# Two convolution layers of a diffusion trunk: the order of the input projection's tiles, and the output projection block by block

## The chip, the core and the metric

The kernel runs on one core of one Trainium2 chip. The metric is device time in microseconds (us) of one execution; lower is better. Three runs of the kernel before took 3041.77, 3048.72 and 3049.2 us, median 3048.72. One execution more was profiled; everything called a row below is from it.

## The reference

Four layers are applied to 1152 tokens (128 context tokens, then a latent grid of 16 x 64), 1024 channels each. Layer i takes mixer i mod 3, so layers 0 and 3 are convolution layers, layer 1 is an attention layer, layer 2 a state space layer. The change touches layers 0 and 3 alone. All data is float32.

```python
h = rms_norm(x, norm_w) * (1 + scale) + shift        # shift, scale, gate: silu(cond) @ ada_w + ada_b
v, g, z = split(h @ w_in + b_in, 3)                  # 1024 x 3072
u = v * sigmoid(g)
u = depthwise_conv(u, w_dw, b_dw)                    # 31 taps along the tokens; context and latent apart
u = silu(layer_norm(u, ln_w, ln_b))                  # over the 1024 channels of a token
y = (u * silu(z)) @ w_out + b_out                    # 1024 x 1024
x = x + gate * y
```

After layer 3 a last RMSNorm gives the outputs.

## The kernel before, in words

Channels lie on partitions, 128 at a time (a tile m, 0 to 7), tokens along the free axis in three blocks of 384. A float32 product is made of three matmuls on two-part operands (hi x hi, lo x hi, hi x lo). A *unit* (`unit`, L511 to L520) is one 128-channel output tile for one block: 8 row tiles x 3 matmuls = 24 matmuls of 128x384 (L517, L518, L519) into one buffer of the PSUM pool `mm`, which has three. The weights come 128 columns (512 KB) at a time: a load on SP's DMA queue (L464, three `raw` buffers), then ScalarE writes the high part `wh` (L478) and GpSimd the low part `wl` (L479), two buffers each, one tile ahead of use (`ahead`).

**Input projection of a convolution layer.** For every m there is a g tile, a v tile and a z tile, three units each. ScalarE takes the sigmoid of g (L662), VectorE multiplies it with v out of PSUM into `u` (L670; three `u` buffers in turn), ScalarE writes silu(z) (L684), and each z tile goes to DRAM (`zd`). After v of tile m, its depthwise convolution is put on a list of small steps: 21 taps on VectorE, accumulating in PSUM (`ca`: L819, then L821), 10 taps on ScalarE and GpSimd (`pa`: L809, L813, L814), and the sum of both (`c`, L830). After each unit `tick` writes the next steps of the list into the program. Buffer `u` of tile m is written again by tile m + 3. In layer 0, 32 columns of `ada_w` (the modulation of this and of the next layer) stand between the tiles (`ada_tile`: 16 + 2 small matmuls each; L281 and L284 on VectorE).

`TAIL` sets where z stands: g0 v0 g1 v1 g2 v2 z0 g3 v3 z1 ... g7 v7 z5 z6, and z7 beside the LayerNorm. The convolution of the last tile is cut into its three blocks, so that the LayerNorm of block 0 can start before blocks 1 and 2 are convolved; those go on between the LayerNorm's steps.

**LayerNorm and gate** (`conv_norm`, L750 to L784), a block at a time: sum over channels by matmuls with ones (L692), mean, difference (L766, even tiles on VectorE, odd ones on GpSimd), square (L768), its sum (L769), the reciprocal root by a dozen tiny VectorE operations (L368 to L376), then for each channel tile two VectorE operations (L777, L780, the second with z read back from DRAM, L775), two on ScalarE (L779, L781) and one on GpSimd (L782). The result is the pair `gh`, `gl`.

**Output projection** (`out_proj`, L620 to L638): for the pair of blocks (0, 1), then for block 2, over m: take the weight tile, load the old x (`xm`, L631; in layer 0 all 1152 tokens of the tile, as they are reordered for layer 1), one unit per block, then scale and bias (L602, ScalarE), add (L611, VectorE) and the sum of squares (L340 ScalarE, L341 GpSimd). So the 8 weight tiles come twice a layer. When a group's blocks are done, the next layer's norm of them starts (in layer 3: three transposes a unit, L1586 and L1588, and the final norm).

**What sets the order.** Every engine runs its own queue in a fixed order. That order is made when the program is built: a planner plays the program through on a timeline of its own; the written order is the priority, and an instruction whose inputs or buffers are not there yet can be passed by a later one.

Of the kernel before, what the change touches and what calls it, by code (L numbers as in the profile page):

```python
# [9 lines left out]
F32 = mybir.dt.float32  # L10
# [9 lines left out]
P = 128  # L20
# [16 lines left out]
POOL_LAST = 10, 10  # L37
# [32 lines left out]
TAIL = {0: TAIL0, 3: TAIL3}  # L70


REST = 4
TURN_ACT = (1,), (1,), (0, 1)
VAR_MM = 2


# Columns of the projection of a pair of heads (0: q, 1: k, 2: v, 3: the gate), in three parts.
# [11 lines left out]
def conv_order(l):  # L90
    """The order of the tiles of a convolution layer: (v, g, z) and the columns of ada_w put in between."""
    ada = [("ada", 0, i) for i in range(2 * KT, 3 * KT)] if l == 0 else []
    ada += [("ada", l + 1, i) for i in range(3 * KT)] if l + 1 < DEPTH else []
    out = []
    n = len(ada)
    for m in range(KT):
        out += [("g", m), ("v", m)] + [("z", z) for z in TAIL[l][0][m]]
    tiles = len(out) - 1
    res = out[:1]
    for i, t in enumerate(out[1:]):  # L100
        res.append(t)
        res += ada[i * n // tiles:(i + 1) * n // tiles]
    return res
# [6 lines left out]
# The latent grid has 16 rows of 64 columns. Besides the row order, its tokens are kept in the order of 8 groups of  # L110
# 8 columns, row by row within a group, where every block of 8 x 16 keys or queries is a run of 128 tokens.
# [5 lines left out]
def cols_of_rows(a, b):  # L117
    """The tokens of block b of the column order, from a, the latent tokens in row order."""
# [3 lines left out]
def rows_of_cols(a, b):  # L122
    """The tokens of block b of the row order, from a, the latent tokens in column order."""
# [3 lines left out]
def like(order, a, b):  # L127
    """The latent part of block b, in the shape that order gives."""
# [5 lines left out]
def interleave(a, na, b, nb):  # L134
    """Runs two generators side by side, na and nb steps of them spread evenly, to the end of both."""
# [11 lines left out]
def part(gen, n):  # L147
    """The next n steps of a generator."""
# [12 lines left out]
def also(a, b, n=1):  # L161
    """Generator a, with n steps of b after each of its own."""
# [6 lines left out]
class Kern:  # L169
    def __init__(self, ctx, tc, A, O, depth):  # L170
# [13 lines left out]
        self.h = [None] * NB  # L184
        self.ada_end = lambda: None
# [78 lines left out]
    def ada_tile(self, l, i):  # L264
        """Column i of the 24 of layer l."""
# [77 lines left out]
    def rstd(self, acc, n, eps, times=1.0):  # L343
        """times / sqrt(sum over partitions of acc / n + eps) on every partition."""
# [7 lines left out]
    def rstd_row(self, row, n, eps):  # L352
        """1 / sqrt(row / n + eps) on every partition, of a row that is the same on all of them."""
# [9 lines left out]
    def rsqrt(self, x, n, eps):  # L363
        """1 / sqrt(x / n + eps) of a [128, 3] operand, by Newton's iteration."""
# [14 lines left out]
    def spread(self, y, times=1.0):  # L379
        """y [128, 3], a value per token, as a row of 384 tokens on every partition."""  # L380
# [34 lines left out]
    # All of them stream through the same buffers in the order of their use, loads and splits ahead of it.  # L415
    def weight_specs(self):
# [5 lines left out]
        for l in range(self.depth):  # L422
            kind, j = l % 3, l // 3
            if kind == 0:
# [7 lines left out]
                out += [(w, 2 * D + z * P, P) for z in TAIL[l][1]]  # L432
# [19 lines left out]
            if kind != 2:  # L452
                out += [(w, m * P, P) for g in range(2) for m in range(KT)]
# [29 lines left out]
    def ahead(self, i):  # L483
        """Loads what follows, and splits the next that is to be split."""
# [26 lines left out]
    def unit(self, out, w, h, width=P, first=True, last=True):  # L511
        """out [width, 384] = w^T h over 8 row tiles."""
# [13 lines left out]
    def tick(self):  # L526
        for _ in range(STEPS_A_UNIT):
# [34 lines left out]
    def hb(self, h, b):  # L562
        """Block b of the normed input h of a layer, what is left of its computation first."""
# [56 lines left out]
    def out_proj(self, l, g, bias=None, order=None):  # L620
# [27 lines left out]
    def conv_layer(self, l, j, order, hook=None):  # L648
        nc, tc, h = self.nc, self.tc, self.h
        with tc.tile_pool(name="cp", bufs=1, space=PSUM, reuse_waits="tile") as cp, ExitStack() as stack:  # L650
            cw = stack.enter_context(tc.tile_pool(name="cw", bufs=2, reuse_waits="tile"))
            close = stack.close
            up = [cw.tile([P, ULEN], F32, name=f"u{i}", bufs=1) for i in range(3)]
# [1060 lines left out]
```

## Time and profile before

| | |
|---|---|
| runs | 3041.77, 3048.72, 3049.2 us (median 3048.72) |
| profiled execution | span 3039.6 us from the first to the last instruction; no other time of that execution is given, so 9.1 us below the median is what lies around the span, and the difference between executions |
| busy share of the span | TensorE 92%, VectorE 72%, GpSimd 48%, ScalarE 44% |
| layer 0 | g and v units from 60.4 us, output projection from 451.8, layer 1's first unit at 596.7 |
| layer 3 | first unit at 2531.9 us, output projection from 2879.1, its last matmul ends at 3025.2, end at 3039.6 |

How to read it: the windows view gives, for a stretch of the span, each engine's busy time with its count of instructions, then the TensorE clock that was granted (1.00 is 2.4 GHz, 0.50 is 1.2 GHz), the busy share of the 16 DMA engines and what they moved. Busy TensorE is not TensorE at its peak, since matmuls overlap; counts of matmuls tell more.

### The profile page before, as it was taken

What the parts mean: (1) busy time and instruction counts of PE and PEld (TensorE: products, weight loads), DVE (VectorE), ACT (ScalarE), POOL (GpSimd) and SP (SyncE); (2) the same over time, 40 slices, a digit from 0 to 9 for tenths busy, and PEclk for the clock granted to TensorE, in tenths of its full rate; (3) what the DMA queues carried; (4) which work ended last, traced back from release to release, by engine and by line L of the source; (5) the groups of instructions that cost most, each with busy time, mean ns of one, the idle gap of its engine ahead of it and who ended that gap; (6) DMA issues with size and microseconds to landing.
All of it is one profiled execution on the core that took longest, in us unless ns stands there. A gap on an engine that the chain in (4) does not pass through costs nothing. (4 is left out here: it accounts for less than half of the span.)

```text
span 3039.6 us, 47664 instructions
## 1 busy us (share of the span) xinstructions
PE 2806.9 (92%) x18263; PEld 2579.5 (85%) x18263; DVE 2174.9 (72%) x3297; ACT 1337.5 (44%) x2293; POOL 1447.8 (48%) x815
## 2 busy tenths in 40 slices
PE   7989988899999999998999999788788999999877
PEld 5979977889999998797999988677677889999677
DVE  5878897754455445557887678987997575999975
ACT  5545555443333334444433334333443444555553
POOL 1767766511111010353134335755675446888764
PEclk7989999999999999998999999999889999999999
DMA  6555424733322333363345579756787863111234
GB/s 215 196 190 153 125 89 128 236 89 92 87 76 75 88 86 86 118 191 112 92 145 165 165 231 289 221 185 211 239 258 223 251 187 96 53 58 56 75 102 137
DMA packets 548643, 445.99 MB, mean 147 GB/s; under 512 B 26944, under 2 KB 506176, under 8 KB 548416
## 3 DMA queue, kind: packets, MB, share of 16 engines
q1 hardware_dynamic: 530704, 422.22, 45.7%
q10 hardware_dynamic: 17712, 20.73, 2.1%
q8 instruction: 144, 2.36, 0.3%
q14 instruction: 83, 0.68, 0.1%
HBM read 337.44 MB, written 101.09 MB: 144 GB/s over the span
## 5 line engine op out<-in xcount | busy, mean ns | idle before, releaser
L479 POOL TENSOR_TENSOR wl<-raw,wh 128x1024 fp32r<-128x1024 f32 x169 | 409.4, 2424 | 959.0 <-ACT wh L478 934.0
L821 DVE SCALAR_TENSOR_TENSOR ca<-u,vec,ca 128x1167 f32<-128x1167 f32 (+4 forms) x420 | 481.4, 1146 | 11.4
L814 POOL TENSOR_TENSOR pa<-pa,pt 128x1167 f32<-128x1167 f32 (+4 forms) x189 | 399.9, 2118 | 87.0 <-ACT pt L813 44.6
L478 ACT CAST wh<-raw 128x1024 fp32r<-128x1024 f32 (+1 forms) x239 | 249.3, 1043 | 313.1 <-issue 61.1
L517 PE MATMUL in_ps<-hh,wh 128*128 128x384 f32 x768 | 268.2, 351 | 4.5 <-ACT hh L408 2.1
L519 PE MATMUL in_ps<-hh,wl 128*128 128x384 f32 x768 | 262.0, 341 | 0.0
L518 PE MATMUL in_ps<-hl,wh 128*128 128x384 f32 x768 | 261.4, 340 | 0.7 <-DVE hl L409 0.7
L813 ACT ACTIVATE pt<-u,vec 128x1167 f32<-128x1167 f32 (+4 forms) x189 | 193.9, 1038 | 108.9 <-POOL pa L814 105.2
L517 PE MATMUL op<-gh,wh 128*128 128x384 f32 x576 | 203.8, 356 | 13.0 <-ACT gh L781 11.0
L1365 DVE SCALAR_TENSOR_TENSOR sca<-ub,vec,sca 128x1155 f32<-128x1155 f32 x144 | 204.9, 1423 | 3.5
L517 PE MATMUL x_ps<-hh,wh 128*128 128x384 f32 x576 | 205.1, 356 | 1.3 <-ACT ub L1316 0.7
L518 PE MATMUL op<-gl,wh 128*128 128x384 f32 x576 | 202.6, 352 | 2.0 <-POOL gl L782 2.0
L519 PE MATMUL op<-gh,wl 128*128 128x384 f32 x576 | 200.9, 350 | 2.2 <-POOL wl L479 2.2
L519 PE MATMUL x_ps<-hh,wl 128*128 128x384 f32 x576 | 197.3, 343 | 0.1
L518 PE MATMUL x_ps<-hl,wh 128*128 128x384 f32 x576 | 196.0, 340 | 0.0
L517 PEld LDWEIGHTS in_ps<-hh,wh 128*128 128x128 f32 x768 | 145.1, 189 | 14.5 <-issue 4.2
L341 POOL TENSOR_TENSOR ssq<-ssq,sq 128x384 f32<-128x384 f32 x84 | 92.6, 1104 | 122.4 <-ACT sq L340 119.2
L519 PE MATMUL op<-sgh,wl 128*128 128x384 f32 x384 | 135.3, 352 | 16.9 <-DVE wl L479 10.9
L518 PEld LDWEIGHTS in_ps<-hl,wh 128*128 128x128 f32 x768 | 145.3, 189 | 2.9 <-DVE hl L409 0.9
L519 PEld LDWEIGHTS in_ps<-hh,wl 128*128 128x128 f32 x768 | 145.2, 189 | 3.1 <-issue 2.4
L611 DVE TENSOR_TENSOR xr<-nt,xm 128x384 f32<-128x384 f32 (+2 forms) x72 | 84.2, 1185 | 85.0 <-ACT nt L605 50.8
L519 PE MATMUL sz_ps<-hh,wl 128*128 128x384 f32 x384 | 137.0, 357 | 7.0 <-DVE wl L479 6.9
(291 smaller groups left out, 8055.0 us busy)
## 6 DMA issues: line engine op xcount, KB each, us to landing
raw<-in_ada_w SPq DMA_DIRECT2D x96, 512.0 KB, 5.1
raw<-in_ssd_w_in SPq DMA_DIRECT2D x62, 512.0 KB, 4.6
raw<-in_conv_w_in SPq DMA_DIRECT2D x48, 512.0 KB, 3.7
raw<-in_ssd_w_out SPq DMA_DIRECT2D x48, 512.0 KB, 4.8
xm<-xs SPq DMA_DIRECT2D x32, 576.0 KB, 4.2
rw<-ssd_rows SPq DMA_DIRECT2D x36, 512.0 KB, 6.6
raw<-in_conv_w_out SPq DMA_DIRECT2D x32, 512.0 KB, 4.1
raw<-in_na_w_in SPq DMA_DIRECT2D x32, 512.0 KB, 4.1
```

The costliest lines, as they stand in the source:

```text
L341: nc.gpsimd.tensor_tensor(out=acc, in0=acc, in1=sq, op=ALU.add)
L478: nc.scalar.copy(out=wh[:, :, :width], in_=s)
L479: self.w_eng.tensor_tensor(out=wl[:, :, :width], in0=s, in1=wh[:, :, :width].bitcast(F32), op=ALU.subtract)
L517: nc.tensor.matmul(out, lhsT=wh[:, k, :width], rhs=hh[:, k, :], start=f, stop=False)
L518: nc.tensor.matmul(out, lhsT=wh[:, k, :width], rhs=hl[:, k, :], start=False, stop=False)
L519: nc.tensor.matmul(out, lhsT=wl[:, k, :width], rhs=hh[:, k, :], start=False, stop=l)
L611: nc.vector.tensor_tensor(out=o, in0=i, in1=x, op=ALU.add)
L813: nc.scalar.activation(out=pt, in_=u_t, func=AF.Copy, scale=wt(t))
L814: nc.gpsimd.tensor_tensor(out=p, in0=p, in1=pt, op=ALU.add)
L821: nc.vector.scalar_tensor_tensor(out=c, in0=u_t, scalar=wt(t), in1=c, op0=ALU.mult, op1=ALU.add)
L1365: nc.vector.scalar_tensor_tensor(out=ca, in0=u[:, t:t + SCLEN], scalar=wt(t), in1=ca, op0=ALU.mult, op1=ALU.add)
```

## The change

In both convolution layers:

1. All g and v tiles come first (with layer 0's `ada_w` columns between them), and the eight z tiles after v7.
2. Six steps instead of four are written into the program after a unit (`CONV_STEPS`), back to four once the list is empty.
3. The last tile's convolution is no longer cut into blocks. The first part of the LayerNorm of all three blocks (sums, differences, squares) stands between z units, the second part of block 0 beside the last seven z units, that of blocks 1 and 2 beside the output projection. All three sums of squares lie in the PSUM space of `ca`. Block 0's pair `gh`, `gl` gets space of its own, and its last z tile is taken from SBUF.
4. The output projection goes block by block, (0), (1), (2): the 8 weight tiles are loaded and split three times instead of twice, and `xm` of a tile comes three times. `xm` uses the buffers of the g and z tiles.

```diff
-TAIL0 = ([(), (), (0,), (1,), (2,), (3,), (4,), (5, 6)], (7,), 0, 10)
-TAIL3 = ([(), (), (0,), (1,), (2,), (3,), (4,), (5, 6)], (7,), 1, 10)
+CONV_STEPS = 6
+LN_STEPS = 2
+Z_LAST = 7
 def conv_order(l):
...
     for m in range(KT):
-        out += [("g", m), ("v", m)] + [("z", z) for z in TAIL[l][0][m]]
+        out += [("g", m), ("v", m)]
...
-    return res
+    return res + [("z", z) for z in range(KT)]
 # weight_specs
-                out += [(w, m * P, P) for g in range(2) for m in range(KT)]
+                out += [(w, m * P, P) for g in range(3 if kind == 0 else 2) for m in range(KT)]
 # out_proj
-            for grp in ((0, 1), (2,)):
+            for grp in grps:
...
-                        xm[m] = pool.tile([P, x1 - x0], F32, name="xm", tag="xm", bufs=2)
+                        if xmp is None:
+                            xm[m] = pool.tile([P, x1 - x0], F32, name="xm", tag="xm", bufs=2)
+                        else:
+                            xm[m] = xmp.tile([P, T], F32, name="xm", tag="sg", bufs=2)[:, :x1 - x0]
 # conv_layer
+            self.steps_a_unit = CONV_STEPS
+            zs = []
...
-                    first, *rest = self.dwconv(cw, cp, u, cb, j, m, order, split=(m == KT - 1))
-                    self.steps += first
+                    self.steps += self.dwconv(cu, cp, u, cb, j, m, order)
...
                 elif t[0] == "z":
-                    for _ in z_tile(m):
-                        pass
+                    zs.append(z_tile(m))
...
-            rest = run(chain(*rest))
-            lns[0] = also(lns[0], rest, REST)
-            z, nz = chain(*[z_tile(m) for m in TAIL[l][1]]), NB * len(TAIL[l][1])
-            interleave(part(z, TAIL[l][2]), TAIL[l][2], part(lns[0], 9), 9)
-            for _ in rest:
-                pass
-            lns[0] = also(lns[0], part(lns[1], 9))
-            interleave(part(lns[0], TAIL[l][3]), TAIL[l][3], z, nz - TAIL[l][2])
-            self.flush()
-            close()
+            z, nz = chain(*zs), KT * NB
+            while self.steps:
+                next(z)
+                nz -= 1
+            self.steps_a_unit = STEPS_A_UNIT
...
             with tc.tile_pool(name="lz", bufs=3, reuse_waits="tile") as self.lz:
+                g0 = [self.lz.tile([P, KT, BW], F32R, name=f"g{i}0", bufs=1) for i in "hl"]
+                g = [None] * NB
+                self.var = cp.tile([P, 3 * 512], F32, name="var", tag="ca", bufs=1)
+                lns = [self.conv_norm(b, j, cb[b], s1, sums, zd, g, cp, g0 if b == 0 else None) for b in range(NB)]
+                firsts = chain(*(part(n, 1 + KT + LN_STEPS) for n in lns))
+                interleave(part(z, nz - Z_LAST), nz - Z_LAST, firsts, NB * (1 + KT + LN_STEPS))
+                interleave(z, Z_LAST, part(lns[0], KT + LAG - LN_STEPS - 1), KT + LAG - LN_STEPS - 1)
+                self.flush()
                 for _ in lns[0]:
                     pass
                 self.gens += lns[1:]
-                self.out_proj(l, g, bias=("conv_b_out", j * KT), order=order)
+                self.out_proj(l, g, bias=("conv_b_out", j * KT), order=order, grps=((0,), (1,), (2,)), xmp=cw)
 # conv_norm
+            if b == 0 and k == KT - 1:
+                z = self.zlast[:, :BW]
+            else:
...
```

## Rows read from the trace of the kernel before

**Rows 1.** The page: span, and busy time with its share of the span and instructions.

```profile
span 3039.6 us, 47664 instructions
...
PE 2806.9 (92%) x18263; PEld 2579.5 (85%) x18263; DVE 2174.9 (72%) x3297; ACT 1337.5 (44%) x2293; POOL 1447.8 (48%) x815
```

**Rows 2.** Windows: stretch, length, busy PE PEld DVE ACT POOL, clock, DMA share, GB/s.

```profile
60.40:451.80 391.40, 368.15 (x2394) 341.25 (x2392) 329.63 (x413) 202.83 (x282) 267.09 (x135) 0.97 0.46 143
451.80:596.70 144.90, 123.70 (x634) 115.63 (x634) 106.19 (x160) 76.58 (x144) 95.24 (x65) 0.93 0.57 177
2531.90:2879.10 347.20, 335.23 (x1823) 318.29 (x1822) 304.27 (x329) 192.74 (x234) 271.54 (x127) 0.99 0.19 58
2879.10:3039.60 160.50, 129.90 (x700) 121.15 (x700) 104.01 (x173) 71.15 (x124) 91.74 (x63) 0.89 0.41 129
```

**Rows 3.** Windows: shorter stretches of both layers.

```profile
158.70:197.50 38.80, 27.83 (x162) 24.62 (x162) 25.24 (x25) 18.08 (x20) 24.97 (x10) 0.78 0.66 211
220.80:263.20 42.40, 42.40 (x295) 40.55 (x293) 37.24 (x37) 23.12 (x26) 33.39 (x14) 1.00 0.56 162
2703.30:2742.00 38.70, 38.70 (x221) 38.17 (x221) 34.76 (x31) 22.34 (x23) 31.49 (x12) 1.00 0.19 62
2838.00:2879.10 41.10, 30.54 (x105) 19.11 (x104) 37.80 (x64) 24.70 (x48) 27.18 (x24) 0.92 0.06 20
552.80:594.00 41.20, 35.03 (x179) 33.00 (x179) 33.73 (x67) 20.96 (x39) 23.24 (x13) 0.92 0.76 240
2988.10:3025.20 37.10, 34.55 (x203) 33.98 (x202) 24.71 (x42) 15.94 (x22) 21.53 (x13) 0.95 0.55 179
3025.20:3039.60 14.40, 1.72 (x13) 1.18 (x11) 4.95 (x17) 2.34 (x3) 0.99 (x1) 0.64 0.27 110
```

**Rows 4.** Timeline of VectorE, one tile's convolution in layer 3: start, duration, instruction, idle before.

```profile
2779.45 1.55 DVE L830 TENSOR_TENSOR c<-ca,pa 128x128 f32<-128x128 f32 x4
2781.03 1.44 DVE L819 TENSOR_SCALAR ca<-u,vec 128x1167 f32<-128x1167 f32 x1
2782.51 14.70 DVE L821 SCALAR_TENSOR_TENSOR ca<-u,vec,ca 128x1167 f32<-128x1167 f32 x10
2798.95 0.74 DVE L670 SCALAR_TENSOR_TENSOR u<-v_ps,vec,sg 128x128 f32<-128x128 f32 x2 [1.75 <-PE v_ps L519]
```

**Rows 5.** Timeline of VectorE, the first tap of each layer.

```profile
88.54 1.44 DVE L819 TENSOR_SCALAR ca<-u,vec 128x1167 f32<-128x1167 f32 x1
...
2560.13 1.44 DVE L819 TENSOR_SCALAR ca<-u,vec 128x1167 f32<-128x1167 f32 x1
```

**Rows 6.** Timeline of VectorE in layer 3's LayerNorm, the last tile's taps beside it.

```profile
2855.14 0.67 DVE L371 TENSOR_SCALAR nr_y<-nr_y 128x3 int32<-128x3 int32 x1
2855.72 0.61 DVE L821 SCALAR_TENSOR_TENSOR ca<-u,vec,ca 128x384 f32<-128x384 f32 x1
2856.24 0.65 DVE L374 SCALAR_TENSOR_TENSOR nr_z<-nr_y,nr_a 128x3 f32<-128x3 f32 x1
```

**Rows 7.** Groups of layer 3 by line and shape: count, busy us, mean ns.

```profile
L814 POOL TENSOR_TENSOR pa<-pa,pt 128x1167 f32<-128x1167 f32 x63 | 171.4, 2721 | 19.9 <-ACT pa L809 15.6 <-ACT pt L813 1.3
L479 POOL TENSOR_TENSOR wl<-raw,wh 128x1024 fp32r<-128x1024 f32 x38 | 93.2, 2456 | 66.7 <-ACT wh L478 66.5
L341 POOL TENSOR_TENSOR ssq<-ssq,sq 128x384 f32<-128x384 f32 x22 | 23.6, 1073 | 28.7 <-ACT sq L340 27.5 <-PE op L519 1.2
```

**Rows 8.** Waits in layer 3: us in total, times, longest.

```profile
DVE u L670 <- PE v_ps L519: 23.7, 17, 4.6
```

**Rows 9.** Chain that ended last, layer 3: start, us, what.

```profile
2832.13 1.29 PE s L692 x4
...
2838.78 4.47 DVE c L766 x4
```

**Rows 10.** One line's instructions in layer 3: duration ns minimum/median/maximum.

```profile
L780 DVE TENSOR_TENSOR c<-c,zk x24: 542/802/2180, 2876.0 to 2958.1; 128x384 f32<-128x384 f32 x24
...
L782 POOL TENSOR_TENSOR gl<-c,gh x24: 992/1319/2253, 2879.2 to 2963.7; 128x384 fp32r<-128x384 f32 x24
```

More of the change, by code (lines that the diff above doesn't have):

```diff
@@ L526, in tick @@
     def tick(self):
-        for _ in range(STEPS_A_UNIT):
+        for _ in range(self.steps_a_unit):
             if not self.steps:
@@ L649, in conv_layer @@
         nc, tc, h = self.nc, self.tc, self.h
[L650 to L653, printed above, removed]
+        with tc.tile_pool(name="cp", bufs=1, space=PSUM, reuse_waits="tile") as cp, \
+                tc.tile_pool(name="cw", bufs=2, reuse_waits="tile") as cw, ExitStack() as stack:
+            cu = stack.enter_context(tc.tile_pool(name="cu", bufs=2, reuse_waits="tile"))
+            up = [cu.tile([P, ULEN], F32, name=f"u{i}", bufs=1) for i in range(3)]
             for u in up:
@@ L693, in sums @@
                                      stop=(k == KT - 1))
-            tiles = conv_order(l)
-            for t in tiles:
+            self.steps_a_unit = CONV_STEPS
+            zs = []
+            for t in conv_order(l):
                 m = t[-1]
@@ L784, in conv_norm, with dwconv @@
         g[b] = gh, gl
-    def dwconv(self, cw, cp, u, cb, j, m, order, split=False):
+    def dwconv(self, cw, cp, u, cb, j, m, order):
         nc = self.nc
@@ L820, in dve @@
             else:
-                nc.vector.scalar_tensor_tensor(out=c, in0=u_t, scalar=wt(t), in1=c, op0=ALU.mult, op1=ALU.add)
-        def end(b):
-            for s0, s1, w in segs(b):
-                i = slice(tok(b, s0) + (0 if w else CPAD), tok(b, s1) + (0 if w else CPAD))
-                o, a0, a1 = cb[b][:, m, s0:s1], ca[:, i], pa[:, i]
-                if order is not None and not w:
-                    o = like(order, o, b)
-                    a0, a1 = (order(a[:, CTX + CPAD:], b) for a in (ca, pa))
-                nc.vector.tensor_tensor(out=o, in0=a0, in1=a1, op=ALU.add)
@@ L832, in steps @@
-        def steps(b):
-            out = []
-            for i in range(nd):
-                out += [lambda f=f, t=i: dve(f, t) for f in views(b)]
-                for q in range(i * np_ // nd, (i + 1) * np_ // nd):
-                    out += [lambda f=f, t=nd + q: pool(f, t) for f in views(b)]
-            return out + [lambda c=c: end(c) for c in (range(NB) if b is None else (b,))]
-        return [steps(b) for b in (range(NB) if split else (None,))]
+                nc.vector.scalar_tensor_tensor(out=ca, in0=u_t, scalar=wt(t), in1=ca, op0=ALU.mult, op1=ALU.add)
@@ new lines, in end @@
+        def end():
+            for b in range(NB):
+                for s0, s1, w in segs(b):
+                    i = slice(tok(b, s0) + (0 if w else CPAD), tok(b, s1) + (0 if w else CPAD))
+                    o, a0, a1 = cb[b][:, m, s0:s1], ca[:, i], pa[:, i]
+                    if order is not None and not w:
+                        o = like(order, o, b)
+                        a0, a1 = (order(a[:, CTX + CPAD:], b) for a in (ca, pa))
+                    nc.vector.tensor_tensor(out=o, in0=a0, in1=a1, op=ALU.add)
@@ L843, in na_tables @@
+        out = []
+        for i in range(nd):
+            out.append(lambda t=i: dve(t))
+            out += [lambda t=nd + q: pool(t) for q in range(i * np_ // nd, (i + 1) * np_ // nd)]
+        return out + [end]
     def na_tables(self, j, pool):
```

63 lines of the change are left out of this document (23 added, 40 removed).

## The prediction

> **What bounds the kernel now.** The page comes first: TensorE is busy for 92% of the span [rows 1], so time can be won only where it idles or waits. The windows view, cut at the two convolution layers, shows where that is [rows 2]. Up to the output projection TensorE is nearly full (368 of 391 us, 335 of 347). In the output stage it is busy for 124 of 145 us in layer 0 and 130 of 160 in layer 3, at a granted clock of 0.93 and 0.89, in which stretches at the lower of the two levels (1.2 and 2.4 GHz) are averaged in. The finer windows give the yardstick [rows 3]: in 38.7 us of full layer 3 there are 221 matmuls, that is nine units of 24, four for two channel sums, and one of the next unit. Two sums take 1.3 us [rows 9], so a unit takes (38.7 - 1.3) / 9 = 4.16 us. A layer's 24 output units are 100 us at that pace. They took 451.8 to 594.0 and 2879.1 to 3025.2, that is 142 and 146 us: some 45 us lost in each, and before it the LayerNorm of layer 3 ran 41.1 us with 105 matmul records [rows 3]. There VectorE is busy for 37.8 us, with the last tile's taps between the LayerNorm's small steps [rows 6]. What ends last in this stage is VectorE, behind it GpSimd, not TensorE.
>
> VectorE in a full cycle (g, v, z of one tile) [rows 4]: first tap 1.48 us, 20 taps at 1.47 (29.4), the sum 1.6, three v products 2.1 (0.74 and two of an estimated 0.65): 34.6 us, against 38.7 of TensorE. Without its three z units TensorE needs 26.3.
>
> **The change part by part.** The sum is made against the profiled span of 3039.6 us and then put on the median, which lies 9.1 us above it.
>
> *Order of g, v, z.* Nothing is computed more or less; TensorE's cycle falls to 26.3 us in layer 3. In layer 0 each `ada_w` column adds 0.9: the window of 42.4 us holds nine units, two sums and 75 small matmuls, which are 4.2 columns in the 3.7 us left [rows 3]. So VectorE, at 34.6 (layer 0: 36.5, with an estimated 1.9 for the columns' small VectorE operations), becomes the slower one. Whether that stops TensorE hangs on the three `mm` buffers, which are free only after L670. I take it that L670 is let in between taps as soon as v is there: each tap needs the one before, and where two chains were ready, VectorE took them in turn, small step, tap, small step [rows 6]. Then the next limit is `u`: v of tile m + 3 needs the taps of tile m done, so TensorE may lead by two tiles. v7 is due after five convolutions, 2560.1 [rows 5] + 5 x 34.6 = 2733; TensorE gets there at 2560 + 40 units x 4.16 + 10 sums x 0.65 = 2733. So it hardly waits, and the z units then run beside convolutions 5 to 7.
>
> *Six steps a unit.* A tile has 33 steps now, and six units write 36. That costs nothing itself; it keeps the list from growing while no z unit empties it.
>
> *GpSimd in a cycle*: nine adds of 2.72 and two `wl` of 2.46 [rows 7] are 29.4 us, with some 3 us before the first add, under VectorE's 34.6. If it were late, convolution 7 would end later by that, at most some 5 us in layer 3 and covered in layer 0.
>
> *Where the output stage starts.* Layer 0: from 60.4, 72 units (299.5), 32 columns (28.8), 48 sums and square sums at 0.65 (31.2), small matmuls (4, estimated), and the stall after v2, where the attention tables' DMAs delay the weights: the 38.8 us window holds 162 matmuls, four units, two sums and 3.4 columns, 21.0 us of work, so 17.8 are lost [rows 3]. That stall follows v2 in both orders; it now meets g3 instead of z0. Its bounds are 0 and 30; I keep 17.8. Together 441.7. Convolution 7 ends at 88.5 [rows 5] + 7 x 36.5 + 32.5 + 17.8 = 394, so the LayerNorm (40 us before) is covered by z. The output stage starts at 442 instead of 452, but with taps, sums and squares of all blocks done. Layer 3: from 2560.1, 66 units and 14 sums end z at 2844. Convolution 7 ends at 2560.1 + 7 x 34.6 + 32.5 = 2835, so here the LayerNorm is not covered. TensorE has 26 us of sums left after z (34 x 0.65 + 4), so not before 2870; by the old chain, 2838.8 [rows 9] to 2879.1 with taps between, it is 2835 + 1 + 40 = 2876 at most. I take 2872.
>
> *The output stage.* Eight more weight tiles a layer: 8 x 2.46 us on GpSimd [rows 7], eight casts on ScalarE (idle half the time), eight loads of 512 KB on SP's queue, and in layer 0 eight more `xm` of 590 KB. An `xm` load waits for a buffer, that is for L611 two units back, and the next weight load queues behind it on SP. This is exactly what block 2 does now, so its pace is the price: 41.2 us for eight units in layer 0 with two norms beside it (5.15 a unit), 37.1 in layer 3 (4.64) [rows 3]. The lower bound is the full pace, 4.16. The upper is today's mean of the whole stage, 145 us / 24 = 6.05. Block 0 has the LayerNorm of two blocks beside it; I take 5.6, between 5.15 and 6.05. Layer 0: 8 x 5.6 + 16 x 5.15 = 127.2. Layer 3: block 1 as dear as layer 0's, 44.8 + 41.2 + 37.1 = 123.1.
>
> *Sums.* Layer 0: 441.7 + 127.2 + 2.7 (from 594.0 to 596.7) = 571.6, 25 us earlier. Layer 3: 2872 + 123.1 + 14.4 for the tail [rows 3] = 3009.5, 30 us earlier. Together 55: span 2985, median 2994. Late next is GpSimd with VectorE in the output stage.
>
> **Weighed against the Trainium skill.** The page SBUF — State Buffer, section "Who interferes with whom", says that a VectorE operation with two SBUF inputs and a GpSimd operation lock each other out of a shared port for a whole instruction. The trace: L780 takes 0.54 us at least and 0.80 in the middle, L782 0.99 and 1.32 [rows 10], so they do slow each other, though by less than one whole instruction each time. By the rule in full, the output stage's GpSimd and VectorE work would add up, and it would stay near its old length, 3034 in all, the first rival below. By the row it is the 5.15 to 5.6 taken, 2994 in all.
>
> **The rivals.**
>
> *The output stage stays at 6.05 a unit.* For it: GpSimd has 24 x 2.46 + 24 x 1.07 [rows 7] + 16 x 1.3 = 106 us of work there, beside VectorE's adds. Against it: blocks 1 and 2 have no taps and no sums of squares beside them. Layer 0 ends at 441.7 + 145.2 + 2.7 = 589.6 (7 gained), layer 3 at 2872 + 145.2 + 14.4 = 3031.6 (8 gained): 3034.
>
> *VectorE holds TensorE in step (the slower side).* If L670 stands behind the sixteen taps written ahead of it, the three `mm` buffers stay taken, and TensorE goes through g and v at VectorE's pace. For it: L670 did stand behind eleven taps and VectorE waited 1.75 us for v [rows 4], 23.7 us in a layer [rows 8]. Against it: there v was late, not VectorE. At 34.6 us a cycle, g and v of layer 3 end at 2802, 21.5 z units are left (89.4), 26 of sums, 123.1 and 14.4: 3055, 15 late. Layer 0, at 36.5: 88.5 + 255.5 + 17.8 + 89.4 + 26 + 127.2 + 2.7 = 607, 10 late. With 3.0 us of waits a cycle (23.7 / 8) it is 36 and 31. So 26 to 68, middle 3096; it decides from about 33 us a cycle on.
> The Trainium skill speaks for this case: TensorE: Matmul & The Clock Gate, "Architectural detail: the array is 16x 32x32, not 1x 128x128", says that VectorE's queue is strictly first in, first out, so a late order is never mended at run time. No row here speaks against the rule; by rows 6 the order made at build time is the better one.
>
> *The planner moves nothing.* The order on the queues is not the written one; it could put z units among g and v again, and the LayerNorm where it was. Against it: weights have two buffers in written order. Then 3049.
>
> **How the numbers follow.** The forecast has 0.58, with a range of its own of 2955 to 3015 (5.15 and 4.64 a unit in all blocks, z's end at 2870 and no stall give 90 less than now; a stall of 30 and a start at 2876 give 39 less). The 6.05 case has 0.20, the case in step 0.13, no effect 0.09. The range to 3050 leaves out the case in step. About 0.3%, 9 us, is what a measurement can tell from no change: faster are the first two, 0.78; the same 0.09; slower 0.13.
>
> **What would show it.** Right: between v7 and the output stage TensorE full with z units; VectorE's taps back to back from the first tile to the eighth; L670 close behind its v unit; the output stage at 442 and 2872, 127 and 123 us long with the last units. Wrong: gaps of some 8 us in each g and v cycle, ended by L670, with a lower granted clock; or z done and TensorE idle over 10 us before the first output unit; or output units at 6 us with waits for `wl`.

## The result, and the profile after

The changed kernel takes 3117.82 us (median of 4 runs, 3115.02 to 3121.75); the kernel before, run beside it, 3045.61. The ratio is 1.0252, with a 95% interval of 1.0232 to 1.0272: slower, where I had forecast 2994 us and a gain. The page of the profile after, span and busy time, against [rows 1]:

```profile
span 3116.7 us, 47576 instructions
...
PE 2811.3 (90%) x18263; PEld 2581.9 (83%) x18263; DVE 2193.0 (70%) x3192; ACT 1314.1 (42%) x2239; POOL 1471.0 (47%) x786
```

TensorE does the same work and is busy 4.4 us longer; the other 72.7 of the 77.1 us are idle time. The windows of the kernel after, cut at the same events as [rows 2] (columns as there), with layer 3 cut further:

```profile
60.30:481.20 420.90, 381.29 (x2425) 353.24 (x2424) 327.90 (x382) 189.87 (x256) 272.59 (x118) 0.95 0.44 136
481.20:641.50 160.30, 119.65 (x605) 111.17 (x604) 115.84 (x140) 80.95 (x143) 99.24 (x62) 0.90 0.67 205
2569.60:2778.30 208.70, 207.30 (x1178) 203.46 (x1177) 182.84 (x182) 101.50 (x105) 164.00 (x65) 1.00 0.18 54
2778.30:2823.10 44.80, 44.69 (x249) 42.98 (x248) 43.74 (x38) 25.29 (x29) 38.69 (x15) 1.00 0.24 80
2823.10:2877.60 54.50, 2.93 (x5) 1.18 (x4) 53.05 (x43) 21.00 (x18) 43.01 (x17) 0.54 0.06 17
2877.60:2965.70 88.10, 86.73 (x425) 74.15 (x426) 35.31 (x68) 34.11 (x68) 34.07 (x24) 0.98 0.20 69
2965.70:3116.70 151.00, 122.39 (x671) 116.39 (x670) 105.70 (x131) 70.84 (x117) 98.38 (x60) 0.91 0.49 152
```

Line 3 holds all g and v units of layer 3: TensorE is full and done with v7 after 208.7 us. Line 4: ten z units, full. Line 5 is the surprise: 54.5 us in which TensorE does 2.9 us of work. Line 6 then holds the other fourteen z units, now on the path. The timeline of the kernel after, TensorE and VectorE at that place (start, duration, instruction, idle before and what ended it):

```profile
2822.76 0.34 PE L514 MATMUL z_ps<-hh,wl 128*128 128x384 f32 x1
2845.06 2.93 PE L690 MATMUL s<-c,ones 128*128 128x384 f32 x4 [21.95 <-DVE c L817]
2877.65 8.64 PE L690 MATMUL s<-c,ones 128*128 128x384 f32 x20 [29.66 <-DVE c L817]
...
2844.38 1.55 DVE L817 TENSOR_TENSOR c<-ca,pa 128x128 f32<-128x128 f32 x4
...
2847.44 29.43 DVE L807 SCALAR_TENSOR_TENSOR ca<-u,vec,ca 128x1167 f32<-128x1167 f32 x20
2876.97 1.55 DVE L817 TENSOR_TENSOR c<-ca,pa 128x128 f32<-128x128 f32 x4
```

TensorE waits at the channel sums of tile 6, then of tile 7, for convolutions that VectorE is still computing tap after tap; fourteen z units that need neither stand behind these sums in its queue. The first five of them had both halves of their weights by then: five z tiles' `wl` were made, the last ending at 2821.0, and the next cast started at 2903.2, behind a z unit. In the output stage of layer 0 (481.2 to 641.5) these are TensorE's largest waits (us in total, times, longest):

```profile
PE rs_ps L385 <- DVE dg L381: 13.5, 2, 7.0
PE op L512 <- ACT wh L473: 11.9, 5, 5.1
PE op L514 <- POOL wl L474: 8.2, 7, 2.5
```

Weights' high and low halves late, 20.1 us; before, the same stage waited 2.2 us for `wl` and 0.6 for `wh`.

### The profile page after: what moved, and what is told of

Same layout as the page of the kernel before. It is cut to its first block, busy times and chain, and to the rows that moved or that the text cites. A ratio compares the mean times of both kernels' runs of the same rounds, so it can differ in the third digit from the quotient of the medians.

```text
span 3116.7 us, 47576 instructions
## 1 busy us (share of the span) xinstructions
PE 2811.3 (90%) x18263; PEld 2581.9 (83%) x18263; DVE 2193.0 (70%) x3192; ACT 1314.1 (42%) x2239; POOL 1471.0 (47%) x786
## 5 line engine op out<-in xcount | busy, mean ns | idle before, releaser
L474 POOL TENSOR_TENSOR wl<-raw,wh 128x1024 fp32r<-128x1024 f32 (+1 forms) x185 | 448.3, 2424 | 1017.0 <-ACT wh L473 984.0
L807 DVE SCALAR_TENSOR_TENSOR ca<-u,vec,ca 128x1167 f32<-128x1167 f32 x320 | 459.6, 1436 | 8.9
L800 POOL TENSOR_TENSOR pa<-pa,pt 128x1167 f32<-128x1167 f32 x144 | 389.4, 2704 | 71.7 <-ACT pa L795 52.8
L473 ACT CAST wh<-raw 128x1024 fp32r<-128x1024 f32 (+1 forms) x255 | 265.8, 1042 | 336.2 <-issue 66.8
L799 ACT ACTIVATE pt<-u,vec 128x1167 f32<-128x1167 f32 x144 | 182.5, 1270 | 155.8 <-POOL pa L800 151.3
L512 PE MATMUL op<-gh,wh 128*128 128x384 f32 x576 | 205.4, 357 | 21.6 <-ACT wh L473 11.9
L606 DVE TENSOR_TENSOR xr<-nt,xm 128x384 f32<-128x384 f32 (+2 forms) x72 | 94.1, 1324 | 83.3 <-ACT nt L600 50.0
L512 PE MATMUL sz_ps<-hh,wh 128*128 128x384 f32 x384 | 139.6, 363 | 8.7 <-DVE nt L1369 7.6
```

The source lines that it names most:

```text
L473: nc.scalar.copy(out=wh[:, :, :width], in_=s)
L474: self.w_eng.tensor_tensor(out=wl[:, :, :width], in0=s, in1=wh[:, :, :width].bitcast(F32), op=ALU.subtract)
L512: nc.tensor.matmul(out, lhsT=wh[:, k, :width], rhs=hh[:, k, :], start=f, stop=False)
L606: nc.vector.tensor_tensor(out=o, in0=i, in1=x, op=ALU.add)
L799: nc.scalar.activation(out=pt, in_=u[:, t:t + CLEN], func=AF.Copy, scale=wt(t))
L800: nc.gpsimd.tensor_tensor(out=pa, in0=pa, in1=pt, op=ALU.add)
```

## The experiments

The table has the length in us of the stages of each profiled run: from the first g unit of a layer to its first output unit ("to out"), and from there to layer 1's first unit (layer 0) or to the end of the span (layer 3). The ratio is to the kernel before, run beside it on the same chip. Two runs are single executions and have their time instead. A stage's length is that of one execution: layers 1 and 2, which all these kernels run alike, took from 1924.9 (e2) to 1939.7 us (e7), so a difference of a few us in one stage shows little.

| run | L0 to out | L0 out | L3 to out | L3 out | ratio (95%) |
|---|---|---|---|---|---|
| before | 391.4 | 144.9 | 347.2 | 160.5 | 1 |
| after | 420.9 | 160.3 | 396.1 | 151.0 | 1.0252 (1.0232 to 1.0272) |
| e1_z_first | 423.8 | 155.4 | 373.1 | 151.3 | 1.0162 (1.0128 to 1.0196) |
| e2_z_all_l3 | 425.3 | 160.2 | 353.7 | 163.8 | 1.0165 (1.0136 to 1.0194) |
| e3_two_passes | 426.0 | 135.1 | 398.3 | 143.9 | 1.0197 (1.0164 to 1.0230) |
| e4_before_blocks | 388.4 | 173.1 | 344.6 | 182.2 | 1.0145 (1.0116 to 1.0174) |
| e5_xm_few | 426.4 | 161.7 | 397.4 | 156.7 | 3136.1 us |
| e6_ada_spread | 426.1 | 152.8 | 397.4 | 151.5 | 3122.8 us |
| e7_repaired | 423.3 | 133.8 | 359.3 | 147.7 | 1.0108 (1.0075 to 1.0140) |
| e8_before_later_z | 402.6 | 143.5 | 356.6 | 159.6 | 1.0065 (1.0040 to 1.0090) |
| e9_all_repaired | 403.2 | 134.4 | 358.6 | 149.5 | 1.0003 (0.9991 to 1.0015) |
| e10_before_whole_conv | 386.1 | 148.0 | 349.2 | 160.2 | 1.0002 (0.9993 to 1.0012) |
| e11_wl_on_vector | 424.1 | 132.0 | 395.8 | 137.7 | 1.0139 (1.0123 to 1.0154) |
| e12_before_z_ahead | 396.7 | 145.8 | 344.4 | 160.8 | 1.0026 (1.0014 to 1.0037) |
| e13_mended_blocks_wl | 403.6 | 131.1 | 356.1 | 143.6 | 0.9954 (0.9938 to 0.9970) |
| e14_mended_two_wl | 401.4 | 129.9 | 359.4 | 143.5 | 0.9968 (0.9959 to 0.9978) |
| e15_before_wl | 390.5 | 140.4 | 347.0 | 155.7 | 0.9956 (0.9942 to 0.9969) |
| e16_before_blocks_wl | 391.7 | 148.4 | 347.1 | 159.7 | 0.9989 (0.9977 to 1.0000) |
| e17_sub_on_vector | 404.1 | 132.5 | 358.9 | 144.1 | 0.9956 (0.9941 to 0.9971) |

### Where z stands: e1, e2

```diff
-            for _ in part(z, 1):
+            for _ in part(z, nz - Z_LAST):     # e1; in e2 all of z, layer 3 alone
                 nz -= 1
             stack.close()
...
+            # e2 too: the sums of tile 6 are deferred by 12 units in layer 3 instead of 2
```

> Edit: in both convolution layers 17 z units are written ahead of the whole LayerNorm (before: 7, and the other 10 interleaved with it); 7 still come after it. Nothing else. Theory A (TensorE's order was made for convolutions 6 and 7 that end earlier than they do, so TensorE waits at their channel sums with z units behind): in layer 3 the wait at the sums of tile 6 stays, some 28 us, because these still stand in the middle of the z units, but the 29.7 us at the sums of tile 7 go, since 8 z units now stand ahead of them; first output unit of layer 3 near 2927 instead of 2965.7, the median about 3080 (3070 to 3095). Layer 0 within 5 us. Theory B (z units 12 and up could not have run: SP stood 50.5 us in front of three zk loads and GpSimd had no further split weights): TensorE then waits for wh or wl inside the z units, first output unit within 10 us of 2965.7, median 3108 to 3120.

> Edit: in layer 3 alone all 24 z units are written ahead of the LayerNorm and the sums of tile 6 come ten units later; layer 0 as in the changed kernel. Theory A: no idle time of TensorE over 3 us between the last v unit and the sums of tile 7, z from 2779 to 2880 in one piece, LayerNorm uncovered for some 30 us after it, first output unit near 2910 instead of 2965.7, median about 3063 (3050 to 3080). Theory B: as for the run before, 3108 to 3120. If the LayerNorm without z units beside it takes over 45 us, first output unit at 2925 or later and 3080.

Measured: in e1 the first output unit comes 23.0 us earlier in layer 3 (373.1 against 396.1), not 39. The wait of e1, then the sums of tile 6 (their second half) and of tile 7 in its timeline, then its window:

```profile
PE s L690 <- DVE c L817: 26.3, 2, 24.9
```

```profile
2850.59 0.81 PE L690 MATMUL s<-c,ones 128*128 128x384 f32 x2
2876.79 3.57 PE L690 MATMUL s<-c,ones 128*128 128x384 f32 x5 [24.88 <-DVE c L817]
```

```profile
2565.00:2938.10 373.10, 343.54 (x1853) 321.90 (x1852) 315.57 (x328) 181.78 (x219) 280.20 (x120) 0.96 0.19 58
```

It is the other way round than theory A had it: the sums of tile 6 now come behind seventeen z units, without a wait, and TensorE waits 24.9 us at those of tile 7, with the last seven z units behind them. That a sum holds up the z units behind it stands; which sum, I had wrong. In e2, with all z units ahead, this wait goes too, and with it 42.4 us of the way to the output stage:

```profile
PE op L512 <- ACT gh L780: 6.1, 1, 6.1
PE s L690 <- DVE c L818: 1.9, 1, 1.9
```

Theory B falls: the weights for those z units were to be had, although SP's queue did stand 50.5 us in front of the `zk` loads. But e2 is no faster than e1. The LayerNorm now has no z units beside it, and the output stage of layer 3 is 12.8 us longer: TensorE waits 9.2 us there for `gh`, which it did not in the kernel after, and 21.3 instead of 13.7 for the adds. The time lost behind the sums was real; this speaks for leaving some z units for the LayerNorm, though no run varies that alone.

### The third pass: e3, e4, e5, e11

```diff
# e3: after                                      # e4: before
-grps=((0,), (1,), (2,))                         -grps=((0, 1), (2,))
+grps=((0, 1), (2,))                             +grps=((0,), (1,), (2,))
# e5: after                                      # e11: after
+if m > 1: xm[m] = old[m % 2]; continue          +self.w_eng = nc.vector      # in out_proj
```

> Edit: the changed kernel with the output projection in two passes over its weights (blocks 0 and 1 together, then block 2) as before the change. Theory C (the third pass, with its eight more wh, wl and weight loads a layer, makes the output stage long): the output stage of layer 0 falls from 160.3 us to about 143, that of layer 3 from 137.2 to about 130, TensorE's waits for wh and wl in it from 25 to under 10 us; median about 3094. Theory A alone: the third pass costs under 5 us in all, since the idle 52 us ahead of the LayerNorm of layer 3 stay; 3112 to 3122. A third way: block 1's LayerNorm is now needed two units after the start and TensorE waits for it some 10 us in each layer; 3115 to 3140.

> Edit: the kernel before with the output projection alone block by block, in three passes over its weights. Theory C: slower than before by 15 to 25 us in layer 0 and 5 to 15 in layer 3, median 3066 to 3085. Theory A alone: within 8 us of before. A gain is possible: block 1's LayerNorm is needed six units later, which takes away TensorE's waits of 6.5 and 5.5 us for it in layer 0; then 3030 to 3040.

> Edit: the changed kernel, but the old x is loaded for the first two column tiles of each block only (6 loads a layer instead of 24), and these two are added for all the others; so part of the residual sum is left out. Theory D (in the output stage the weight loads queue on SP behind loads of the old x, which wait for an add on VectorE that frees one of two buffers): the output stage of layer 0 falls from 160.3 us to 140 or less, TensorE's waits for wh and wl in it from 20 to under 8 us; layer 3, whose loads are a third as large, from 142 to 136. Theory C' (the casts on ScalarE and the subtractions on GpSimd of the eight more weight tiles are what is late): both stages within 5 us of the changed kernel's.

> Edit: the changed kernel with the low halves wl of the output projection's weights made on VectorE (1.22 us each where it does this in layer 2) instead of GpSimd (2.4 us). Theory C'1 (GpSimd is late with wl, and the cast wh behind it): the output stage of layer 0 falls from 160.3 us to 145 or less, the waits for wh and wl from 20 us to under 6; layer 3 from 142 to about 137; median some 20 us less than the changed kernel. Theory C'2 (only two buffers of split weights, so each tile's cast waits for the unit two back, whoever makes wl): waits for wh stay at 10 us or more, both stages within 6 us. Theory C'3 (what is late are the next layer's norms, whose rs_ps stands in TensorE's order ahead of output units): the 13.5 us at rs_ps stay or grow, since VectorE gets 30 us more work.

Measured: taking the third pass out of the changed kernel shortens layer 0's output stage by 25.2 us and layer 3's by 7.1. Putting it alone into the kernel before lengthens them by 28.2 and 21.7 us, more in both than I had set for theory C. The waits of e4 in layer 0's output stage:

```profile
PE op L517 <- ACT wh L478: 14.9, 7, 5.3
PE op L519 <- POOL wl L479: 9.1, 8, 1.9
```

Theory D (loads of the old x in the weights' way) falls: with a quarter of these loads, and the DMA share down from 0.67 to 0.45, layer 0's stage stays at 161.7 us; layer 3's is 156.7. Theory C'1 stands: with `wl` made on VectorE the two stages lose 28.3 and 13.3 us, more than by leaving the pass out, though VectorE has 24 instructions more. The waits for `wh` and `wl` fall to 8.9 us (I had set under 6), and the median falls by 35 us where I had set some 20. The waits of e11 in layer 0's output stage:

```profile
PE rs_ps L385 <- DVE dg L381: 8.4, 2, 5.3
PE op L514 <- DVE wl L474: 5.4, 3, 2.1
PE op L512 <- ACT wh L473: 3.5, 3, 1.6
```

Why VectorE is better off with more work is seen at its add of the old x in layer 3's output stage, first in the kernel after, then in e11 (duration in ns minimum/median/maximum, first and last start):

```profile
L606 DVE TENSOR_TENSOR fx<-nt,xm x31: 276/2245/2583, 2971.4 to 3099.6; 128x384 f32<-128x384 f32 x15, 128x128 f32<-128x128 f32 x8, 128x256 f32<-128x256 f32 x8
```

```profile
L606 DVE TENSOR_TENSOR fx<-nt,xm x31: 276/551/1229, 2946.4 to 3060.1; 128x384 f32<-128x384 f32 x15, 128x128 f32<-128x128 f32 x8, 128x256 f32<-128x256 f32 x8
```

The same add takes 2.2 us beside GpSimd's `wl` and 0.55 without it. One such pair in the timeline of the kernel after, GpSimd and VectorE:

```profile
549.25 2.39 POOL L474 TENSOR_TENSOR wl<-raw,wh 128x1024 fp32r<-128x1024 f32 x1 [0.80 <-ACT wh L473]
...
549.77 2.28 DVE L606 TENSOR_TENSOR xr<-nt,xm 128x384 f32<-128x384 f32 x1 [3.10 <-ACT nt L597]
```

The add starts while `wl` runs and ends at 552.05, some 0.4 us after `wl` (551.64), as if it had waited for the end of that instruction. It is no single case: of the 51 such adds in the two output stages that start while GpSimd is at work, 49 end between 0.15 and 0.48 us after GpSimd's instruction, and the twelve that meet none take 0.41 to 0.56 us. The Trainium skill (SBUF — State Buffer, "Who interferes with whom") says that a VectorE operation with two SBUF inputs contends with a GpSimd operation that reads SBUF, by an exclusive lock, and that issue order decides who blocks. These rows agree. How much of e11's gain is this, and how much GpSimd's own lateness with `wl`, no run separates.

### Layer 0 and the sum of the losses: e6, e7, e9

```diff
# e6: after, conv_order: the columns stand between all 24 tiles, z too
-    tiles = len(out) - 1
+    out += [("z", z) for z in range(KT)]
+    tiles = len(out) - 1
# e7: e6 with e3's two passes; layer 3 with 21 z units ahead, the sums of tile 6 ten units later
# e9: e7 with 17 z units ahead in layer 0 too
```

> Edit: the changed kernel, with the 32 ada_w columns of layer 0 spread over all 24 tiles (g, v and z), as before the change over nearly all, instead of over the 16 g and v tiles. Theory E (two columns instead of one and a half a tile take the raw weight buffers, so that the next weight load comes late whenever DMA or GpSimd slips; that is what lengthened layer 0 up to the output stage): TensorE's idle time from the first g unit to the first output unit falls from 39.2 us to 25 or less and the stage from 420.9 us to about 400, with the granted clock of 100 to 120 and 220 to 260 back at 1. Rival (the stalls come from g and v units being twice as dense, whose weights meet the taps on GpSimd, and from the tables' DMAs): the stage stays within 6 us of 420.9. Layer 3 unchanged.

> Edit: the changed kernel with three things undone or mended: columns spread as in the run before, the output projection in two passes, and in layer 3 21 z units ahead of the LayerNorm with the sums of tile 6 ten units later. If the three losses add up: layer 0 from first g to layer 1 about 545 us (changed: 581.2, before: 536.3), layer 3 from first g to the last matmul about 500 (537.9 and 497.4), together some 70 us less than the changed kernel, ratio to before 1.000 to 1.006. If they share a cause (the weights' path), less than 50 us are gained, ratio over 1.009. Faster than before by over 0.3% only if the z units at the end had been right in themselves.

> Edit: the run e7_repaired, and in layer 0 too 17 z units ahead of the LayerNorm (e7: 7 or 8). In e7 TensorE waited 21.5 us in layer 0 for the sums of tile 7, in its order ahead of z units. Theory A: this wait goes to under 5 us, layer 0 from first g to layer 1 falls from 557.1 us to about 537, ratio to before near 1.004 (1.001 to 1.007); the new order repaired is no faster than the old one. Rival (layer 0 is held by weights and by the ada_w columns among the z units): the wait comes back as waits for wl or ada_sb, and layer 0 stays over 550.

Measured: e6, a single execution, brings v7 of layer 0 to 242 us after the first g unit instead of 275, and yet the output stage starts no earlier (426.1 us, within what the rival had set). Up to v7 TensorE idles 9.7 us instead of 28.3; the rest of the 33 us is columns that now stand among the z units. The wait comes back at the sums of tile 7, which layer 0 in the changed kernel had met with only 3.1 us:

```profile
PE s L696 <- DVE c L826: 21.5, 1, 21.5
```

So theory E fits the idle time of the g and v stage and fails for the whole: a TensorE that is earlier meets the same order. In e9 the z units stand ahead of that sum, the wait is gone, and layer 0 takes 403.2 us to its output stage, 20.1 less than in e7:

```profile
58.80:462.00 403.20, 379.07 (x2424) 346.66 (x2422) 328.26 (x381) 193.28 (x258) 274.01 (x119) 0.97 0.45 141
```

With the order, the columns and the pass mended the loss is gone: e9 is at 1.0003, as fast as before and no faster. e7 missed its expected 1.000 to 1.006, and its 1.0108 lies where I had put a shared cause of the losses (over 1.009); e9, one edit further, shows that what e7 lacked was layer 0's 21.5 us. Even e9 is not mended in full: in layer 3 TensorE still waits at the sums of tile 7, with three z units behind them (12.1 us here, 10.3 in e13).

```profile
2848.24 8.80 PE L696 MATMUL s<-c,ones 128*128 128x384 f32 x20 [12.09 <-DVE c L827]
```

### What of it is worth doing in the old order: e8, e10, e12

```diff
# e8
-TAIL3 = ([(), (), (0,), (1,), (2,), (3,), (4,), (5, 6)], (7,), 1, 10)     # TAIL0 alike
+TAIL3 = ([(), (), (), (0,), (1,), (2,), (3,), (4, 5)], (6, 7), 1, 10)
# e12: e8, and three of the last six z units ahead of the LayerNorm's first sums
# e10: before
-dwconv(cw, cp, u, cb, j, m, order, split=(m == KT - 1))
+dwconv(cw, cp, u, cb, j, m, order, split=False)
```

> Edit: the kernel before, in both layers one more z tile after the last v (tiles 6 and 7 instead of 7), the others one g, v pair later. By my theory of TensorE's order: convolution 7 ends some 8 us earlier in layer 3 (four to five us of TensorE's lead a z unit), the three more z units cover the LayerNorm, where TensorE idled 12 us in layer 3 and 23 in layer 0, and the kernel gains 5 to 20 us, ratio 0.993 to 0.998. Rival (any z unit that is not needed to keep TensorE busy ahead of the last v is written where the plan puts the sums in front of it): ratio 1.000 to 1.008.

> Edit: the kernel before with the convolution of the last tile in one piece, as the change has it, instead of block by block. Theory F (the block split lets the LayerNorm and output of block 0 run beside the taps of blocks 1 and 2; whoever gives it up pays some 10 us a layer): first output unit 8 to 15 us later in each layer, part of it given back in an output stage without taps, median 5 to 20 us above before, ratio 1.002 to 1.007. Rival (the split only costs smaller instructions): 0 to 8 us faster.

> Edit: the run e8_before_later_z, with three of its six last z units written ahead of the last taps and the LayerNorm's first sums. In e8 TensorE waited 8.7 us in layer 3 at the channel sums of block 0 of tile 7, z units behind it. Theory A: this wait goes, layer 3 and layer 0 each 6 to 10 us shorter than in e8 (506.8 and 546.0), ratio to before 0.999 to 1.003. Rival (a z unit after the last v always lengthens the way to the output stage, because it takes TensorE between the LayerNorm's sums): as e8, ratio 1.004 to 1.009.

Measured: one z tile later costs 0.65% (e8), where I expected a gain. In its layer 3 TensorE waited 8.7 us at the sums of tile 7's block 0. With three z units ahead of them (e12) most of it is back and 0.26% are left. Where, the profile of e12 does not show: it was its fastest execution (3041.4 us, median 3049.44), with layer 0 up to layer 1's first unit 6.2 us longer than before and layer 3 2.5 shorter. The block split of the last convolution is worth nothing that can be measured (e10); theory F falls.

### The version that beats both: e13 to e17

```diff
# e13: e9 with three passes, e14: e9 with two, e15: before, e16: e4; each with
             self.out_begin(l, bias, pool)
+            self.w_eng = nc.vector               # back to nc.gpsimd at the end
# e17: e13, and in conv_norm
-(nc.gpsimd if k % 2 else nc.vector).tensor_tensor(out=c[:, k, :], ... op=ALU.subtract)
+nc.vector.tensor_tensor(out=c[:, k, :], ... op=ALU.subtract)
```

> Edit: the run e9_all_repaired, but with the output projection block by block again (three passes) and wl of its weights made on VectorE. If GpSimd's subtractions are the whole price of the third pass: output stages of 132 us in layer 0 and 129 in layer 3 (as in e11) behind e9's 403 and 359, together 1023 us against 1036.6 in e9, ratio to before 0.995 to 0.998, the changed order then a gain. If the third pass still costs something by its loads and casts: both stages at 138 us or more, ratio 0.999 to 1.003.

> Edit: the run e9_all_repaired with wl of the output projection's weights made on VectorE, two passes. If the third pass is free once GpSimd is relieved: within 5 us of e13. If it still costs: 5 to 15 us less than e13, ratio 0.992 to 0.997. If in two passes wl was never late (waits for wh and wl were 2.2 us in layer 0 of the run with two passes): within 4 us of e9, ratio 0.999 to 1.002.

> Edit: the kernel before with wl of the convolution layers' output weights made on VectorE, nothing else. TensorE waited 2.2 us for wl in layer 0's output stage and 8.0 for gh behind ScalarE. If the gain of e11 belongs to the third pass alone: within 6 us of before, ratio 0.998 to 1.002. If GpSimd is what the output stage of before waits for: 10 to 20 us less, ratio 0.993 to 0.997. VectorE has the last taps and the LayerNorm beside it there, so a loss is possible: 1.002 to 1.006.

> Edit: the run e4_before_blocks (the kernel before with the output projection alone in three passes) with wl made on VectorE. In e4 TensorE waited 14.9 us for wh and 9.1 for wl in layer 0's output stage. If these were GpSimd's: the 28 and 23 us that the third pass cost in the two layers go to under 8 each, ratio 0.998 to 1.005. If loads and casts of the eight more tiles are late by themselves: over 1.008.

> Edit: the run e13_mended_blocks_wl, with the 24 subtractions c - mu of each LayerNorm all on VectorE instead of twelve there and twelve on GpSimd side by side. Theory L (a two-input VectorE operation and a GpSimd operation on SBUF take turns: side by side VectorE's took 1.35 us, the first, alone, 0.56): 24 subtractions take 13 to 14.5 us on VectorE alone, no longer than the 15.4 that the divided work took; first output unit 0 to 3 us earlier in each layer, ratio to before within 0.002 of e13's 0.9954. Rival (the two engines do work in parallel, and 1.35 us is what such a subtraction costs): 24 x 1.35 = 32 us, first output unit some 10 us later in layer 3, where the LayerNorm is not covered, ratio 0.998 or more.

Measured: e13 takes 0.46% less than before, e15 0.44%. The windows of e13, cut as those of the kernel after:

```profile
60.20:463.80 403.60, 379.06 (x2425) 346.40 (x2423) 327.52 (x382) 193.27 (x258) 272.84 (x118) 0.97 0.45 141
463.80:594.90 131.10, 114.69 (x607) 110.81 (x606) 105.95 (x166) 78.96 (x141) 46.99 (x38) 0.93 0.78 254
2525.50:2881.60 356.10, 341.13 (x1853) 320.00 (x1852) 309.40 (x325) 180.11 (x215) 272.74 (x114) 0.99 0.19 59
2881.60:3025.20 143.60, 120.25 (x671) 115.95 (x670) 99.36 (x158) 73.90 (x121) 53.67 (x44) 0.92 0.52 166
```

In the changed order no price of the third pass is left to be measured once GpSimd is relieved (e13 against e14: the intervals overlap). With two passes, too, moving `wl` gains (e14 against e9, 0.9968 against 1.0003). In the old order it keeps a small price, 0.9989 against 0.9956 (e16, e15), 8.0 us in layer 0's output stage and 4.0 in layer 3's. The gain is not the change's: that one edit in the old kernel (e15) gives as much as the changed order with its order mended and the same edit (e13).

e17 measures the turn-taking by itself. The 24 subtractions of a LayerNorm took 15.4 us divided between the engines; on VectorE alone, in layer 3, they run from 2848.93 to 2860.80, 11.9 us, a gap of 0.44 included. First the lines and the timeline in the kernel after, then in e17:

```profile
L761 DVE TENSOR_TENSOR c<-c,mu x24: 557/1348/1359, 396.3 to 2893.0; 128x384 f32<-128x384 f32 x24
L761 POOL TENSOR_TENSOR c<-c,mu x24: 1302/1312/1370, 396.4 to 2893.9; 128x384 f32<-128x384 f32 x24
...
2879.86 14.54 DVE L761 TENSOR_TENSOR c<-c,mu 128x384 f32<-128x384 f32 x12 [1.33 <-ACT mu L757]
2879.90 15.37 POOL L761 TENSOR_TENSOR c<-c,mu 128x384 f32<-128x384 f32 x12 [7.95 <-ACT mu L757]
```

```profile
L775 DVE TENSOR_TENSOR c<-c,mu x48: 545/548/559, 401.4 to 2860.2; 128x384 f32<-128x384 f32 x48
...
2848.93 7.59 DVE L775 TENSOR_TENSOR c<-c,mu 128x384 f32<-128x384 f32 x16 [1.34 <-ACT mu L771]
2856.96 3.84 DVE L775 TENSOR_TENSOR c<-c,mu 128x384 f32<-128x384 f32 x8 [0.44 <-ACT mu L771]
```

The time of the kernel stays (0.9956 against 0.9954), as theory L expected; the first output unit does not come earlier, as it also expected, but 0.5 and 2.8 us later in the profiled execution.

## Why the prediction was wrong

By its own stages, the forecast against the changed kernel and against e13:

| stage | forecast | after | off by | e13 |
|---|---|---|---|---|
| layer 0 to output | 381.3 | 420.9 | +39.6 | 403.6 |
| layer 0 output | 129.9 | 160.3 | +30.4 | 131.1 |
| layers 1 and 2 | 1935.2 (as before) | 1928.1 | -7.1 | 1930.6 |
| layer 3 to output | 340.1 | 396.1 | +56.0 | 356.1 |
| layer 3 output and tail | 137.5 | 151.0 | +13.5 | 143.6 |

*Order of g, v, z: right up to v7, then the step that failed.* VectorE's pace and TensorE's lead were forecast well. In layer 0 convolution 7 ends at 395.7 (394 forecast); in layer 3, which starts 37.7 us later than before, at 2878.5, or 2840.8 on the old clock (2835 forecast). v7 is done at 2740.6 on that clock (2733). TensorE is full for 207.3 of 208.7 us, so VectorE does not hold it in step: the slower rival had nearly the size (3096), but not the mechanism. What failed is "the z units then run beside convolutions 5 to 7". I followed what each engine could do, not what its queue says. The order is fixed when the program is built; the sums of tile 6 stood after the tenth z unit, those of tile 7 behind them, and TensorE waited 51.6 us there. e1 and e2 show it: with the written order alone changed, 23.0 and 42.4 of the 56.0 us come back. The place of tile 7's sums followed what was written, not when the convolution ends: ten z units stand ahead of them in both layers of the kernel after, with a wait of 3.1 us in layer 0 and 29.7 in layer 3, seventeen in e1, all 24 in e2. Why the plan did not let more z units pass is open; no run shows its own durations. My rival "the planner moves nothing" asked about the order and put a price of zero on it. [Rows 9] already showed the sums as a place where the chain passes from one engine to the other, and I did not ask what would stand behind them. None of my signs of being wrong named this gap; the last of them, output units at 6 us with waits for `wl`, did show.

*Where the output stage starts, layer 0.* I kept the 17.8 us stall and counted the rest as full work. TensorE idles some 40 us there; the `ada_w` columns over 16 tiles instead of nearly all (e6) and the same order (e9) together make up 17.3 of the 39.6 us that I was off. The other 22.3 stay in e13: 24.5 us idle (403.6 less 379.06) instead of 17.8, and 379.06 us of busy time where I had counted 363.5, at a granted clock of 0.97. Most of that idle time is waits at the `ada_w` columns, which the sum had at nothing; of the stall after v2 little is left in e13 (4.3 us idle from 160 to 200, where the kernel after has 11.6). The waits of layer 0 up to its output stage, first before, then e13:

```profile
PE ada_ps L280 <- ACT ada_sb L275: 2.6, 2, 1.5
PE ada_ps L282 <- ACT ada_sb L277: 18.6, 8, 7.7
```

*The output stage: mis-sized.* 6.7 us a unit in layer 0 (160.3 / 24) instead of 5.4, 5.7 in layer 3 (137.2 / 24) instead of 5.13. By blocks it is 7.6, 5.9 and 5.9 in layer 0, where I had 5.6 and twice 5.15, and 6.9, 5.4 and 4.8 in layer 3, where I had 5.6, 5.15 and 4.64 (the blocks start at 481.2, 542.3 and 589.8, and at 2965.7, 3021.2 and 3064.5). Block 0, which has the LayerNorm of the two others beside it, is where I was off most; my yardstick, block 2 of the old order [rows 3], has no such work beside it. And I read [rows 10] as two engines that slow each other "by less than one whole instruction each time", from minima and medians. A minimum shows the pairs that missed each other; the maxima, 2180 and 2253 ns, fit one operation drawn out over the other engine's. The first rival had the right mechanism for this stage; its price, 6.05 a unit, was too low for layer 0 and too high for layer 3. The Trainium skill's rule (SBUF — State Buffer, "Who interferes with whom"), which I had set aside there, describes it: the measured 2.2 us beside `wl` agree with it. With `wl` off GpSimd (e13) the stages come within 1.2 and 6.1 us of my forecast; block 0 of layer 3 still takes 6.9 a unit.

*Six steps a unit, GpSimd in a cycle*: in the trace after VectorE waits for GpSimd's taps once, for 1.1 us in layer 3; no run changes either alone.

## What to carry to other kernels

When work is moved out of an engine's way to fill another's idle time, look up what will stand in front of it in that engine's queue, and what that waits for: a queue in fixed order gives nothing to work that stands behind a late instruction, however ready it is. Write the filler ahead of the instruction that will be late, and see whether the chain that follows needs some of it (e2 gained nothing on e1 by spending it all). Before an elementwise step is given to GpSimd to relieve VectorE, compare VectorE's own medians with its minima; where its two-input operations are drawn out to the length of GpSimd's, the step is cheaper on VectorE.

## What the runs showed of the hardware that I had not expected

Two-input subtractions of 128x384 divided evenly between VectorE and GpSimd were slower than on VectorE alone: 1.35 and 1.31 us each side by side, 0.55 alone, 15.4 us against 11.9 for 24. The low half of a weight tile took 2.4 us on GpSimd and 1.3 on VectorE, and moving it (e11) shortened VectorE's other work by more than that: in layer 3's output stage VectorE's busy time fell from 105.70 to 91.87 us although it had 23 more such instructions. GpSimd's remaining operations became no shorter (in layer 0's output stage `gl` took 1165 ns in the mean, and 1284 in e11).
